# A transformer block with S5 and sparse attention: inputs laid out by the host, the first norm's root by a power on GpSimd

## The chip, the core and the metric

The kernel runs on one core of a Trainium2 chip. The core has five engines that run side by side, each through its own queue in order: TensorE (PE), VectorE (DVE), ScalarE (ACT), GpSimd (POOL) and SyncE (SP), which here only issues transfers. On-chip data lie in SBUF and, for PE's results, in the eight banks of PSUM. The metric is the device time of one execution in microseconds (us), lower is better.

## The reference

One block of a decoder in float32 on 512 tokens of width 1024:

```python
n1 = rmsnorm(h, g_mix)                       # y = x * rsqrt(mean(x*x) + eps) * g
z = n1 @ w_in                                # 1024 x 3864: ssm input, queries, 6 key/value sets, gates, merge
y_ssm = s5_mixer(z[:512], a_re, a_im, log_dt, b, c, d, w_glu)
y_nsa = nsa_mixer(q, kv, gate_logits, ...)   # compressed, selected and window attention, 8 heads
merge = sigmoid(z[1816:])
h = h + (merge[:1024] * (y_ssm @ w_br_ssm) + merge[1024:] * (y_nsa @ w_br_nsa)) @ w_out
h = h + conv_ffn(rmsnorm(h, g_ffn), w_up, conv_w, conv_b, w_down)
h = h + sigmoid(rmsnorm(h, g_ple) @ w_ple_gate) * (p @ w_ple_proj)
out = rmsnorm(h, g_final)
```

The part that matters most here is the start: rmsnorm of x, the product p @ w_ple_proj (the "embedding"), which needs nothing else, the columns of z that hold values and gates, and the parameters of the state space model: dt = exp(log_dt), a_bar = exp(lam * dt) with a complex lam, so that the kernel needs an exponential and the sine and cosine of an angle for each of 32 x 64 states.

## The kernel before

A float32 product is made of three passes in a faster type (helper mm3, lines 83 to 85): each operand is split into a high part, a copy that ACT makes (line 76), and a low part, a subtraction on DVE or POOL (line 55 through `split`). PE multiplies with the contracted dimension on the partitions. So x, p and several small parameter arrays, whose rows lie the other way in memory, are turned by PE transposes through PSUM.

The order of the first stage is written out by hand for PE, ACT and DVE, in a `manual_schedule` block (lines 365 to 441); POOL's order, and the order of all later work, comes from a planner that places each instruction by its own estimate of when it is ready. `issue_after(x)` queues what is traced inside it behind x on x's engine. In the first stage stand:

- g_mix, a row, is spread over the partitions by two products with ones (L368); prow (three parameter rows of the model), drow and p (pin) are transposed (L371, L381, L376).
- The embedding, matmuls `embedded(i, qt)` (L351) with 512 columns, for two halves i of w_ple_proj and four blocks qt of 128 tokens, three passes of two each: 48 in all. `embedded_out` copies the sums from PSUM to SBUF on ACT. The names `acc` and `o` are two PSUM banks each, taken in turn by `either()`.
- Norm 1, for each block: the sum of squares of its rows on ACT (L309; for block 0 half of it on DVE, L388); the root `rstd_of` (lines 120 to 136) as seven or nine small DVE steps; `x_scaled` (L316 on, recorded at L64) multiplies x by the root and by g_mix, on DVE; eight transposes (L324); `t_high` copies the high part n1h from PSUM on ACT; `t_low` makes the low part n1l on DVE from PSUM.
- `v_passes(qt, ...)` (L298): for each block 24 matmuls with 280 columns, which make the values of two attention branches and the gates from n1 and WV; `v_out` takes them out of PSUM (L305 for the gates).
- `u_split` prepares the first two weight tiles of w_in.

Behind that block PE makes four projections `proj` (L83 to L85, group `pj`) for the model's input, eight more for queries, compressed and plain keys, and interleaves the model's own matmuls in four quarters (`ssm_quarter`).

The model's parameters: step exponential `exp_of` with tag e0 and the angles (kk, fl) run on POOL; a second exponential, tag e1, gives rho, also on POOL; both are chains of operations on 128 x 16 elements. On POOL a fused multiply-add is two instructions (`stg`). Behind `trig_at` (the last DVE instruction traced before, that is t_low of block 2), DVE makes sines and cosines (L507 to L536), powers PR and PI, the coefficients bb from B (braw); POOL makes the tables `tab` (L55 in group tab). C (craw) is turned by two groups of four transposes (L591), the gains of the later norms and the compression's position terms by L580 and L582, and the convolution's weights and bias (crow) by four (L1132) at 316 us, between projection matmuls late in the attention stage.

Weights come in tiles of 512 KB by `wraw` (L187), three buffers in turn, on SP's DMA queue. A tile of w_in or w_up is read in pieces of 512 B, the others in pieces of 1 or 2 KB; B is read in pieces of 64 B, C in pieces of 256 B and twice, so that it stands on both halves of the partitions.

Of the kernel before, what the change touches and what calls it, by code (L numbers as in the profile page):

```python
# [18 lines left out]
P = 128  # L19
T = 512  # L20
# [25 lines left out]
def hybrid_kernel(ctx: ExitStack, tc: tile.TileContext, A, out):  # L46
# [186 lines left out]
    sX = ExitStack()
    px = sX.enter_context(pool("x", 1, "right"))
    xall = slot(cp, "h16", [P, NQ, D], F32, "xall")
    xts = [xall[:, qt] for qt in range(NQ)]
    sq = px.tile([P, D], F32, name="sq")
    wv0 = slot(py, "y8", [P, 2, KD, P], F32, "wv0")
    grow = wv0[0:1, 1].rearrange("p a b -> p (a b)")
    ones = pP.tile([1, P], F32, name="ones")  # L240
    G.memset(ones, 1.0)
    grow2 = pP.tile([2 * KD, P], F32, name="grow2")
    gains = cp.tile([P, 2, KD], F32, name="gains")

    def xload(qt):
        nc.sync.dma_start(xts[qt], dr("x", qt * P * D, [[D, P], [1, D]]))


    pin = slot(pa, "v4", [P, NQ, PLE], F32, "pin")
# [5 lines left out]
    def wpload(i):  # L255
        nc.sync.dma_start(wpr[:, i], dr("w_ple_proj", i * 512, [[D, P], [P * D, 2], [1, 512]]))

    nc.sync.dma_start(grow, dr("g_mix", 0, [[D, 1], [1, D]]))
    nc.sync.dma_start(pin, dr("p", 0, [[PLE, P], [P * PLE, NQ], [1, PLE]]))
# [3 lines left out]
    xload(1)  # L263
    nc.scalar.dma_start(dlog, dr("ssm_log_dt", 0, [[2, NPAIR], [1, 2]]))
    nc.scalar.dma_start(prow[:, 0], dr("ssm_a_re", 0, [[P, NPAIR], [1, P]]))
    nc.scalar.dma_start(prow[:, 1], dr("ssm_a_im", 0, [[P, NPAIR], [1, P]]))
    nc.scalar.dma_start(drow, dr("ssm_d", 0, [[P, 4], [1, P]]))
# [3 lines left out]
    VCOLS = ((OFF_KV + 384, 0, P, wv0[:, 0]),  # L271
             (OFF_KV + 640, P, P + 24, slot(py, "t8", [P, KD, P + 24], F32, "wv1")))
    for c0, w0, w, raw in VCOLS:
        nc.sync.dma_start(raw, dr("w_in", c0, [[INW, P], [P * INW, KD], [1, w]]))
    for qt in range(2, NQ):
        xload(qt)
    uraw = [wraw("w_in", INW, 0, ct * P, KD, P) for ct in range(2)]
    for i, nm in enumerate(("g_ffn", "g_ple")):
        nc.sync.dma_start(grow2[i * KD:(i + 1) * KD], dr(nm, 0, [[P, KD], [1, P]]))
# [5 lines left out]
    def wv(x, i):  # L285
        _, w0, w, raw = VCOLS[i]
        return WV[:, x, :, w0:w0 + w], raw
# [20 lines left out]
    def squared(qt):  # L308
        S.activation(sq, xts[qt], AF.Square, accum_out=ss4[:, qt:qt + 1])  # L309

    G.tensor_copy(prow[:, 2].rearrange("p (g s) -> p g s", g=2), dlog[:, :, None].to_broadcast([NPAIR, 2, HD]))
    prm = pP.tile([P, 3, NPAIR], F32, name="prm")

    def x_scaled(qt, r):
        for i, x in enumerate(halves(xts[qt])):
            stt(x, x, r, gbs[i], MUL, MUL)  # L316

    def t_high(qt):

        res = []  # L320
        for b in range(2):
# [1271 lines left out]
```

## Time and profile before

| what | value |
|---|---|
| median of 3 runs (lowest, highest) | 819.1 us (818.9, 819.38) |
| span of the profiled execution, first to last instruction | 817.2 us |
| so outside that span, by the median | 1.9 us |
| PE busy in that span | 802.4 us, 98% |
| DVE, ACT, POOL busy | 523.2, 401.2, 252.0 us |
| instructions | 12276 |
| transfers | 87.85 MB, 114305 packets, 97733 of them between 512 B and 2 KB |
| mean granted PE clock | 0.997 |

The profile is of one execution. L12 stands for line 12 of the kernel; a line can be that of a helper, so that groups are told apart by the names of their tiles. "Busy" for PE counts a pipelined matmul to its modelled end, so that a busy PE is not always at its peak; the step from one start to the next tells its rate.

### The profile page before, as it was taken

How to read it: one execution, taken by the hardware profiler on the slowest of the kernel's cores; microseconds unless marked ns; L12 is line 12 of the kernel's file. 1: busy time of each engine (PE TensorE's matmuls, PEld its weight loads, DVE VectorE, ACT ScalarE, POOL GpSimd, SP SyncE). 2: the span in 40 equal slices, each digit the busy share in tenths (PEclk: the TensorE clock that was granted, in tenths of full speed). 3: DMA queues.
4: the chain of work that ended last, by engine and by line, in shares of the span. 5: the costliest groups of instructions: out<-in, count | busy, mean ns of one | idle time of the engine just before them, and what ended most of it. 6: DMA issues, size and time to landing. Idle time of an engine off the chain costs nothing. (4 is left out here: it accounts for less than half of the span.)

```text
span 817.2 us, 12276 instructions
## 1 busy us (share of the span) xinstructions
PE 802.4 (98%) x4523; PEld 674.4 (83%) x4523; DVE 523.2 (64%) x1085; ACT 401.2 (49%) x746; POOL 252.0 (31%) x309
## 2 busy tenths in 40 slices
PE   8999999999999999999999999999999999999995
PEld 5977888888888888878898888888888888888884
DVE  4899888756777742296444444555444757898764
ACT  5548364435877653334354344444444433484632
POOL 6477021015645444141032322333333200000321
PEclk9999999999999999999999999999999999999998
DMA  9937232422333413345033233332332352525111
GB/s 295 271 102 181 69 88 54 105 78 81 100 78 78 155 53 83 103 154 155 1 92 108 86 102 103 104 96 86 102 99 84 102 177 80 206 67 167 51 52 51
DMA packets 114305, 87.85 MB, mean 108 GB/s; under 512 B 9921, under 2 KB 97733, under 8 KB 114246
## 3 DMA queue, kind: packets, MB, share of 16 engines
q1 hardware_dynamic: 113566, 86.02, 36.5%
q10 hardware_dynamic: 680, 1.07, 0.3%
q8 instruction: 35, 0.57, 0.3%
q14 instruction: 24, 0.20, 0.1%
HBM read 77.63 MB, written 5.24 MB: 101 GB/s over the span
## 5 line engine op out<-in xcount | busy, mean ns | idle before, releaser
L55 POOL TENSOR_TENSOR wl<-wr,wh 128x1024 fp32r<-128x1024 f32 x39 | 93.9, 2407 | 250.0 <-ACT wh L76 249.9
L76 ACT ACTIVATE wh<-wr 128x1024 fp32r<-128x1024 f32 x88 | 93.2, 1059 | 96.8 <-issue 29.2
L55 DVE TENSOR_TENSOR wl<-wr,wh 128x1024 fp32r<-128x1024 f32 x49 | 63.5, 1297 | 56.4 <-ACT wh L76 56.4
L83 PE MATMUL pj<-n1h,wh 128*128 128x512 f32 x224 | 91.0, 406 | 0.6 <-ACT gates L305 0.6
L85 PE MATMUL pj<-n1h,wl 128*128 128x512 f32 x224 | 88.1, 394 | 0.8 <-DVE wl L55 0.8
L84 PE MATMUL pj<-n1l,wh 128*128 128x512 f32 x224 | 87.9, 392 | 0.0
L64 DVE SCALAR_TENSOR_TENSOR cv<-ub,cvp,cv 128x511 f32<-128x511 f32 (+1 forms) x44 | 32.9, 748 | 66.2 <-ACT cv L1272 65.5
L84 PE MATMUL ua<-n2l,wh 128*128 128x512 f32 (+1 forms) x176 | 66.9, 380 | 0.2 <-DVE n2l L64 0.2
L83 PE MATMUL ua<-n2h,wh 128*128 128x512 f32 (+1 forms) x176 | 66.9, 380 | 0.0
L85 PE MATMUL ub<-n2h,wl 128*128 128x512 f32 (+1 forms) x176 | 66.8, 379 | 0.0
L83 PE MATMUL ub<-n2h,wh 128*128 128x512 f32 (+1 forms) x176 | 66.8, 379 | 0.0
L84 PE MATMUL ub<-n2l,wh 128*128 128x512 f32 (+1 forms) x176 | 66.8, 379 | 0.0
L85 PE MATMUL ua<-n2h,wl 128*128 128x512 f32 (+1 forms) x176 | 66.8, 379 | 0.0
L85 PEld LDWEIGHTS pj<-n1h,wl 128*128 128x128 f32 x224 | 42.1, 188 | 10.7 <-DVE wl L55 1.6
L83 PEld LDWEIGHTS pj<-n1h,wh 128*128 128x128 f32 x224 | 42.1, 188 | 8.4 <-ACT gates L305 0.8
L61 POOL TENSOR_SCALAR pr<-pr,su,gates 128x512 f32<-128x512 f32 (+1 forms) x64 | 39.1, 622 | 31.4 <-DVE su L983 28.9
L84 PEld LDWEIGHTS pj<-n1l,wh 128*128 128x128 f32 x224 | 42.2, 188 | 7.5 <-issue 0.4
L55 DVE TENSOR_TENSOR pl<-ptp,ph 128x128 fp32r<-128x128 f32 (+1 forms) x64 | 31.2, 488 | 15.1 <-ACT ph L76 14.7
L55 POOL TENSOR_TENSOR wg1l<-wr,wg1h 128x1024 fp32r<-128x1024 f32 x2 | 4.8, 2424 | 113.6 <-ACT wg1h L76 113.6
L982 ACT ACTIVATE pr<-pr,nb 128x512 f32<-128x512 f32 (+1 forms) x64 | 35.6, 557 | 7.6 <-DVE nb L980 7.5
L76 ACT ACTIVATE ph<-ptp 128x128 fp32r<-128x128 f32 (+1 forms) x64 | 27.7, 433 | 22.8 <-PE ptp L991 22.3
L84 PEld LDWEIGHTS ua<-n2l,wh 128*128 128x128 f32 x176 | 33.1, 188 | 6.7 <-DVE n2l L64 0.4
(500 smaller groups left out, 2077.3 us busy)
## 6 DMA issues: line engine op xcount, KB each, us to landing
wr<-in_w_up_dram SPq DMA_DIRECT2D x44, 512.0 KB, 4.0
wr<-in_w_in_dram SPq DMA_DIRECT2D x28, 512.0 KB, 3.9
b<-in_w_down_dram SPq DMA_DIRECT2D x14, 512.0 KB, 3.7
QQ<-QT SPq DMA_DIRECT2D x16, 256.0 KB, 3.6
wr<-in_w_out_dram SPq DMA_DIRECT2D x8, 512.0 KB, 3.5
wr<-in_w_down_dram SPq DMA_DIRECT2D x8, 512.0 KB, 4.8
wr<-in_w_ple_gate_dram SPq DMA_DIRECT2D x8, 512.0 KB
xall<-in_x_dram SPq DMA_DIRECT2D x4, 512.0 KB
```

Source lines behind the costliest of these rows:

```text
L55: e.tensor_tensor(o, a, b, op=op)
L61: e.tensor_scalar(o, a, s1, s2, op0=op0, op1=op1)
L64: e.scalar_tensor_tensor(o, a, s, b, op0=op0, op1=op1)
L76: S.activation(o, a, AF.Copy)
L83: PE.matmul(ps, lh, rh, start=start, stop=False)
L84: PE.matmul(ps, lh, rl, start=False, stop=False)
L85: PE.matmul(ps, ll, rh, start=False, stop=stop)
L982: S.activation(pp, pp, AF.Exp, bias=nb, scale=-1.0, accum_out=su)
```

## The change

Six things change together.

1. The host hands over copies with another order of the same numbers (`laid_out`). Weight tiles lie in memory as they are loaded, so each partition reads one piece. x comes twice: as rows (for the squares and for the residual) and as x_t, blocks with the model dimension on the partitions. p comes transposed. All parameters that were transposed by PE come as one array of columns, `cols`; B and C as one array `bc`, C already on both halves. The value and gate columns of w_in come as `w_v`.
2. The transposes of x, p, prow, drow, grow2, perow, craw and crow go, with g_mix's spread and their copies from PSUM.
3. Norm 1 works on x_t: x_gain multiplies by g_mix on POOL; rooted, on POOL, adds the two sums, takes the power -0.5 and multiplies a unit matrix by the result; spread, on PE, multiplies that diagonal by a constant matrix, so that each token's root stands on all partitions, in PSUM; x_scaled, n_high and n_low follow on DVE, ACT and DVE.
4. POOL's order in the first stage is written by hand as well.
5. The step exponential and the angles move from POOL to DVE: five steps before the squares of block 0, 21 behind them. The second exponential stays on POOL, queued behind the low part of the second half of w_ple_proj.
6. The order of the block is new (the lines that the old order had are left out below): first passes of the embedding go over all four blocks, all three value passes of a block stand together, v_out of block 0 and 1 come earlier.

```diff
 def wraw(name, ld, row0, c0, kt, c, raw=None):
...
-        nc.sync.dma_start(raw, dr(name, row0 * ld + c0, [[ld, P], [P * ld, kt], [1, c]]))
+        n = (row0 // (kt * P)) * (ld // c) + c0 // c
+        nc.sync.dma_start(raw, dr(name, n * P * kt * c, [[kt * c, P], [c, kt], [1, c]]))
...
+    cols = cp.tile([P, NCOLS], F32, name="cols")
+    gmix, gains, dcol, prm, pes, cvp = (cols[:, a:b] for a, b in zip(COLS, COLS[1:]))
...
+    bcraw = pP.tile([P, 4, NPAIR, 16], F32, name="bcraw")
+    root = px.tile([P, P], F32, name="root")
+    G.memset(root, math.sqrt(D))
+    half = px.tile([P, 1], F32, name="half")
+    G.memset(half, -0.5)
     def xload(qt):
-        nc.sync.dma_start(xts[qt], dr("x", qt * P * D, [[D, P], [1, D]]))
+        nc.sync.dma_start(rows[qt], dr("x", qt * P * D, [[D, P], [1, D]]))
+        nc.sync.dma_start(xT[:, qt], dr("x_t", qt * P * D, [[D, P], [P, KD], [1, P]]))
...
+    nc.scalar.dma_start(cols, dr("cols", 0, [[NCOLS, P], [1, NCOLS]]))
+    for k in range(2):
+        nc.sync.dma_start(pin[:, k], dr("p_t", k * T, [[2 * T, P], [1, T]]))
     wpload(0)
     xload(0)
     wpload(1)
-    xload(1)
...
+    for w0, w, raw in VCOLS:
+        nc.sync.dma_start(raw, dr("w_v", P * KD * w0, [[KD * w, P], [w, KD], [1, w]]))
+    for qt in range(1, NQ):
         xload(qt)
     uraw = [wraw("w_in", INW, 0, ct * P, KD, P) for ct in range(2)]
...
+    def x_gain(qt):
+        tt(xT[:, qt], xT[:, qt], gm8, MUL, G)
+    def rooted(qt, s2=0.0):
+        r = small("rx")
+        ts(r, ss4[:, qt:qt + 1], s2, D * EPS, ADD, ADD, G)
+        tt(r, r, half, ALU.pow, G)
+        dgs[qt] = px.tile([P, P], F32, name="dg", tag="dg", bufs=1)
+        ts(dgs[qt], ident, r, None, MUL, None, G)
+    def spread(qt):
+        if not rbp:
+            rbp[0] = bank("s", "rb")
+        PE.matmul(rbp[0][:, qt * P:(qt + 1) * P], root, dgs[qt], start=True, stop=True)
+    def x_scaled(qt):
+        tt(xT[:, qt], xT[:, qt], rbp[0][:, None, qt * P:(qt + 1) * P].to_broadcast([P, KD, P]), MUL)
+    def n_high(qt):
+        copy(n1h[n_of(qt)], xT[:, qt])
+    def n_low(qt):
+        tt(n1l[n_of(qt)], xT[:, qt], n1h[n_of(qt)], SUB)
...
+    def angles():
+        ts(lre, prm[:, 0], -1e-4, None, ALU.min)
+        yield
+        yield from exp_of(dt, prm[:, 2], "e0", V)
+        tt(lr, lre, dt, MUL)
+        yield
+        tt(th, aim, dt, MUL)
+        yield
+        C0 = 2 * math.pi / 4096
+        c1 = math.floor(C0 * 2 ** 18) / 2 ** 18
+        c2 = math.floor((C0 - c1) * 2 ** 29) / 2 ** 29
+        c3 = C0 - c1 - c2
+        ts(kk, th, 1.0 / C0, MAGIC, MUL, ADD)
+        yield
+        ts(kk, kk, MAGIC, None, SUB)
+        yield
+        stt(fl, kk, -c1, th, MUL, ADD)
+        yield
+        stt(fl, kk, -c2, fl, MUL, ADD)
+        yield
+        stt(fl, kk, -c3, fl, MUL, ADD)
+        yield
+        ts(fl, fl, 1 / (2 * math.pi))
+        yield
+        ts(rd, kk, 1 / 4096.0, MAGIC, MUL, ADD)
+        yield
+        ts(rd, rd, MAGIC, None, SUB)
+        yield
+        stt(kk, rd, -4096.0, kk, MUL, ADD)
+        yield
...
+    with tc.manual_schedule(engines={mybir.EngineType.PE, mybir.EngineType.Activation, mybir.EngineType.DVE,
+                                    mybir.EngineType.Pool}):
         for k in range(2):
+            copy(pT[0][:, k], pin[:, k])
+            tt(pT[1][:, k], pin[:, k], pT[0][:, k], SUB)
+        angled = angles()
+        for _ in range(5):
+            next(angled)
+        for k in range(2):
+            copy(wp[0][:, 0, k], wpr[:, 0, k])
         tt(wp[0][:, 1], wpr[:, 0], wp[0][:, 0], SUB)
+        x0 = halves(rows[0])
+        S.activation(x0[0], x0[0], AF.Square, accum_out=ss4[:, 0:1])
+        V.tensor_tensor_reduce(out=x0[1], in0=x0[1], in1=x0[1], scale=1.0, scalar=0.0, op0=MUL, op1=ADD,
                                accum_out=ss4[:, NQ:])
+        x_gain(0)
+        rooted(0, ss4[:, NQ:])
+        for n in range(2):
+            for k in range(2):
+                for qt in range(NQ):
+                    embedded(0, qt, (n,), (k,))
         copy(wp[1][:, 0], wpr[:, 1])
+        copy(*wv(0, 0))
+        for _ in angled:
+            pass
+        spread(0)
+        x_scaled(0)
         tt(wp[1][:, 1], wpr[:, 1], wp[1][:, 0], SUB, G)
+        exp_at = last(mybir.EngineType.Pool)
+        for qt in range(NQ):
+            embedded(0, qt, (2,))
         for qt in range(2):
             embedded_out(0, qt)
+        squared(1)
+        rooted(1)
+        x_gain(1)
+        n_high(0)
+        wv_lo(0)
+        n_low(0)
         for qt in (2, 3):
             embedded_out(0, qt)
+        for qt in range(3):
+            embedded(1, qt)
         squared(2)
+        V.tensor_copy(*wv(0, 1))
+        spread(1)
+        embedded(1, 3)
+        embedded_out(1, 0)
+        x_scaled(1)
+        n_high(1)
+        rooted(2)
+        x_gain(2)
+        wv_lo(1)
+        n_low(1)
         squared(3)
+        for qt in (1, 2):
             embedded_out(1, qt)
+        v_passes(0, (0, 1, 2))
+        spread(2)
+        x_scaled(2)
+        n_high(2)
+        rooted(3)
+        x_gain(3)
+        embedded_out(1, 3)
+        n_low(2)
         trig_at = last(mybir.EngineType.DVE)
+        v_passes(1, (0, 1, 2))
         u_split(0, 0)
+        spread(3)
+        x_scaled(3)
+        v_passes(2, (0, 1, 2))
+        n_high(3)
+        n_low(3)
         u_split(0, 1)
+        v_out(0)
         u_split(1, 0)
         zero_at = last(mybir.EngineType.Activation)
+        u_split(1, 1)
+        v_out(1)
         v_passes(3, (0, 1, 2))
         for qt in (2, 3):
             v_out(qt)
...
+    with tc.issue_after(exp_at):
+        for _ in exp_of(rho, lr, "e1", G):
+            pass
...
-    with tc.issue_after(first_v):
-        ppe = bank("s", "ppe")
-        PE.transpose(ppe[:, 32:32 + 2 * KD], grow2, ident[:2 * KD, :2 * KD])
...
+        copy(FL[:, i, :, :, NCMP - 1], pes[:, i, :, None].to_broadcast([P, 16, 2]))
+        S.activation(CT[:, i], bcraw[:, 2 + i], AF.Copy, scale=(1.0, -1.0)[i])
...
-    for i in range(4):
-        PE.transpose(ps[:, i * 44:(i + 1) * 44], crow[:, i], ident[:44, :44])
-    V.tensor_copy(cvp.rearrange("p a b -> p (a b)"), ps[:, :176])
...
+def laid_out(i):
+    def tiles(w, kt, c):
+        k, n = w.shape
+        return w.reshape(k // (kt * P), kt, P, n // c, c).transpose(0, 3, 2, 1, 4)
...
+        "x_t": x.reshape(NQ, P, KD, P).transpose(0, 3, 2, 1),
+        "p_t": i["p"].reshape(T, 2, P).transpose(2, 1, 0),
+        "cols": np.concatenate(cols, 1),
+        "bc": np.stack(bs + cs, 1),
```

More of the change, by code (lines that the diff above doesn't have):

```diff
@@ L308, in squared, with n_of @@
     def squared(qt):
[L309 to L321, printed above, removed]
-            ps = bank("t", "nt")
-            for k in range(4):
-                PE.transpose(ps[:, k * P:(k + 1) * P], xts[qt][:, (4 * b + k) * P:(4 * b + k + 1) * P], ident)
-            o = (slice(None), slice(4 * b, 4 * b + 4), slice(qt * P, qt * P + P))
-            res.append((o, ps.rearrange("p (k t) -> p k t", k=4)))
-            copy(n1h[o], res[-1][1])
-        return res
-    def t_low(res):
-        for o, ps in res:
-            tt(n1l[o], ps, n1h[o], SUB)
+        S.activation(rows[qt], rows[qt], AF.Square, accum_out=ss4[:, qt:qt + 1])
+    gm8 = gmix[:, :, None].to_broadcast([P, KD, P])
+    rbp = {}
+    dgs = {}
+    def x_gain(qt):
[12 more added lines that the diff above has]
+        tt(xT[:, qt], xT[:, qt], rbp[0][:, None, qt * P:(qt + 1) * P].to_broadcast([P, KD, P]), MUL)
+    def n_of(qt):
+        return (slice(None), slice(None), slice(qt * P, qt * P + P))
+    def n_high(qt):
+        copy(n1h[n_of(qt)], xT[:, qt])
+    def n_low(qt):
+        tt(n1l[n_of(qt)], xT[:, qt], n1h[n_of(qt)], SUB)
     uw = []
@@ L349, in embedded @@
         for n in passes:
-            for k in range(2):
+            for k in ks:
                 PE.matmul(pjb[i, qt], pT[int(n == 1)][:, k, qt * P:(qt + 1) * P], wp[i][:, int(n == 2), k], start=n + k == 0,
@@ L363, in embedded_out @@
         copy(pjo[i, qt], pjb[i, qt])
-    with tc.manual_schedule(engines={mybir.EngineType.PE, mybir.EngineType.Activation, mybir.EngineType.DVE}):
-        gbs = [bank("s", f"gb{i}") for i in range(2)]
-        for ps, g in zip(gbs, halves(grow)):
-            PE.matmul(ps, ones, g, start=True, stop=True)
-        pps = bank("t", "pps")
-        for i in (2, 0, 1):
-            PE.transpose(pps[:, i * 16:(i + 1) * 16], prow[:, i], ident[:NPAIR, :NPAIR])
-        copy(prm.rearrange("p a b -> p (a b)"), pps[:, :48])
-        for k in range(2):
-            ps = bank(either(), "ptr")
-            for qt in range(NQ):
-                PE.transpose(ps[:, qt * P:(qt + 1) * P], pin[:, qt, k * P:(k + 1) * P], ident)
-            copy(pT[0][:, k], ps)
-            tt(pT[1][:, k], ps, pT[0][:, k], SUB)
-        copy(wp[0][:, 0], wpr[:, 0])
-        tt(wp[0][:, 1], wpr[:, 0], wp[0][:, 0], SUB)
-        PE.transpose(pps[:, 48:52], drow, ident[:4, :4])
-        copy(dcol, pps[:, 48:52])
-        for n in range(3):
-            for qt in range(2):
-                embedded(0, qt, (n,))
-        x0 = halves(xts[0])
-        S.activation(sq[:, :512], x0[0], AF.Square, accum_out=ss4[:, 0:1])
-        V.tensor_tensor_reduce(out=sq[:, 512:], in0=x0[1], in1=x0[1], scale=1.0, scalar=0.0, op0=MUL, op1=ADD,
-                               accum_out=ss4[:, NQ:])
-        x_scaled(0, rstd_of(ss4[:, 0:1], ss4[:, NQ:]))
-        copy(wp[1][:, 0], wpr[:, 1])
@@ L1579 @@
     arrays, args = {}, {}
-    for name in _INS:
-        a = _np.ascontiguousarray(inputs[name])
+    for name, a in laid_out(inputs).items():
+        a = _np.ascontiguousarray(a)
         arrays[f"in_{name}_dram"] = a
```

202 lines of the change are left out of this document (66 added, 136 removed).

## The prediction

> **What bounds the kernel now.** I read the page, then busy time by stretch, who PE waited for, and PE in order of time.
>
> ```profile
> span 817.2 us, 12276 instructions
> PE 802.4 (98%) x4523; PEld 674.4 (83%) x4523; DVE 523.2 (64%) x1085; ACT 401.2 (49%) x746; POOL 252.0 (31%) x309
> ```
> ```profile
> 0.00:10.00 10.00, 6.08 (x16) 3.47 (x17) 1.40 (x3) 3.69 (x7) 3.89 (x28) 1.00 0.78 275
> 10.00:40.00 30.00, 30.00 (x184) 27.11 (x185) 26.22 (x72) 19.02 (x38) 18.59 (x56) 1.00 1.11 287
> 40.00:80.00 40.00, 38.57 (x230) 30.80 (x230) 36.90 (x86) 25.15 (x52) 30.93 (x59) 1.00 0.55 143
> 80.00:400.00 320.00, 320.00 (x2164) 270.70 (x2163) 213.70 (x523) 167.18 (x364) 102.20 (x98) 1.00 0.33 92
> 400.00:800.00 400.00, 399.63 (x1877) 334.80 (x1876) 236.69 (x381) 182.22 (x281) 92.51 (x65) 1.00 0.33 100
> ```
> After the stretch and its length stand PE, PEld, DVE, ACT and POOL busy, granted clock, DMA share and GB/s. From 10 to 800 us PE is idle for 1.8 us in all, with DMA at a third after 80 us. The rearranged weights of the later stages are therefore priced at nothing: PE's own work hides their loads, and without that cover a load's saving (0.5 us, from the transfer rates below) would count once per load. The change gains only what it takes from PE, or from PE's waits, and nearly all of that lies before 60 us.
>
> ```profile
> 10.00 2.07 PE L351 MATMUL pje<-wp,pTh 128*128 128x512 f32 x4 [1.44 <-ACT dcol L76]
> 11.87 1.91 PE L351 MATMUL pje<-wp,pTl 128*128 128x512 f32 x4
> 13.58 1.30 PE L351 MATMUL pje<-wp,pTh 128*128 128x512 f32 x4
> 14.72 1.04 PE L324 MATMUL nt<-ident,xall 128*128 128x128 f32 x8
> 15.51 0.70 PE L351 MATMUL pje<-wp,pTh 128*128 128x512 f32 x2
> ...
> 25.85 1.19 PE L298 MATMUL vps<-WV,n1l 128*128 128x280 f32 x8
> 26.88 1.20 PE L298 MATMUL vps<-WV,n1h 128*128 128x280 f32 x8
> ...
> 39.03 0.23 PE L580 MATMUL ppe<-ident,grow 16*128 16x16 f32 x1
> ...
> 39.73 0.48 PE L83 MATMUL pj<-n1h,wh 128*128 128x512 f32 x1
> ```
> Columns: start, length, then what ran. Embedding starts at 10.00 and first steps by 0.43 us a matmul (11.87 to 13.58, four). A value matmul steps by 0.129 (25.85 to 26.88, eight), eight transposes of x take 0.79 (14.72 to 15.51), and the first projection starts at 39.73. The question is where that start goes.
>
> **The change, part by part.** *PE.* Out of the first stage: four groups of transposes of x (3.2 us), 0.70 of ppe and cps (39.03 to 39.73), and all that stands before 10.00. In: four spreads. Their nearest row is four fp32 products of 128 columns, eight passes, in 1.06 us:
>
> ```profile
> 76.69 1.06 PE L718 MATMUL wps<-Uc,WB 128*128 128x128 f32 x8
> ```
> That is 0.27 each; the bounds are 0.22 (the same without the last one's tail) and 0.5 (with a stop at each change of operand type). I take 0.35, so 1.4.
>
> *Transfers.* These rows have the columns of the second fence.
>
> ```profile
> 5.00:10.00 5.00, 3.56 (x14) 2.31 (x13) 1.40 (x3) 2.40 (x6) 2.42 (x10) 1.00 1.03 394
> 20.00:25.00 5.00, 5.00 (x28) 4.16 (x27) 3.39 (x7) 3.60 (x9) 4.02 (x12) 1.00 1.14 129
> ```
> The first holds p, w_ple_proj and x, in pieces of 1 KB and more; the second B and C, in pieces of 64 and 256 B. The new loads all have long pieces, so 394 GB/s holds throughout and 512 KB take 1.33 us. x comes twice: 2 MB more. Counting SP's queue in order (the first 785 KB by 5 us, as before) with 0.7 us for the last packets gives: w_ple_proj half 0 at 6.7, rows of x 0 at 8.0, x_t 0 at 9.4, half 1 at 10.7, w_v at 12.0 and 13.6, then rows and x_t in turn at 14.9, 16.3, 17.6, 18.9, 20.3, 21.6, the first u weights at 22.9. ACT issues one DMA for four, ahead of its work.
>
> *Engines.* For each 128 tokens: a square on ACT; on POOL x_gain (two inputs, 1024 columns), an add, a power and a diagonal; the spread; x_scaled on DVE from PSUM; n_high on ACT; n_low on DVE, whose inputs now both lie in SBUF.
>
> ```profile
> L55 POOL TENSOR_TENSOR wl<-wr,wh 128x1024 fp32r<-128x1024 f32 x39 | 93.9, 2407 | 250.0 <-ACT wh L76 249.9
> L76 ACT ACTIVATE wh<-wr 128x1024 fp32r<-128x1024 f32 x88 | 93.2, 1059 | 96.8 <-issue 29.2
> L55 DVE TENSOR_TENSOR wl<-wr,wh 128x1024 fp32r<-128x1024 f32 x49 | 63.5, 1297 | 56.4 <-ACT wh L76 56.4
> ```
> ```profile
> 12.98 0.22 POOL L55 TENSOR_TENSOR e0q<-gtFalse,e0r 128x16 f32<-128x16 f32 x1
> 13.29 0.25 POOL L59 TENSOR_SCALAR gtFalse<-e0q 128x16 f32<-128x16 f32 x1
> 13.50 2.38 POOL L55 TENSOR_TENSOR wp<-wpr,wp 128x1024 fp32r<-128x1024 f32 x1
> ```
> x_gain is 2.4, x_scaled and n_low 1.2 each, a copy on ACT 1.0 (0.53 for 512 columns). No row has a power. From below it is 0.22 (a multiply), from above 2.4 (the longest POOL row); as its one column is nearest to the short rows I take 0.4, so add, power and diagonal take 1.1. The step exponential and angles (26 small operations) go to DVE: five early, 21 behind the squares. Their price, and what they wait for, shows here:
>
> ```profile
> 381.43 2.41 POOL L55 TENSOR_TENSOR wl<-wr,wh 128x1024 fp32r<-128x1024 f32 x1 [18.92 <-ACT wh L76]
> ```
> ```profile
> 382.38 1.47 DVE L64 SCALAR_TENSOR_TENSOR rt<-ry,rv 128x1 f32<-128x1 f32 x1
> 383.88 0.16 DVE L64 SCALAR_TENSOR_TENSOR rt<-rt 128x1 f32<-128x1 f32 x1
> 384.08 0.16 DVE L64 SCALAR_TENSOR_TENSOR ry<-rt,ry 128x1 f32<-128x1 f32 x1
> 384.27 0.22 DVE L64 SCALAR_TENSOR_TENSOR rt<-ry,rv 128x1 f32<-128x1 f32 x1
> ```
> A chained small step costs 0.2. But the one at 382.38 took 1.47 and ended at 383.85, with POOL's multiply (383.84): a DVE operation with two SBUF inputs stands still while POOL streams. So each x_gain and the low half of w_ple_proj block the angles, wv_lo and n_low, and the reverse.
>
> *The walk.* PE starts at 7.3 (half 0 copied). Sixteen matmuls, nine at 0.43 and seven at 0.23, end at 12.9. POOL has x_gain 9.4 to 11.8, the root until 12.9, the spread follows at once, then the low half of w_ple_proj until 15.1. PE does twenty more and stands at 17.8 before embedded(1, 2): its bank is freed by embedded_out(0, 2), which ACT holds behind n_high(0), behind x_scaled(0), behind the 21 angles. These start at 9.6, need 4.2 us, lose 4.3 to POOL and end at 18.1. x_scaled, n_high and the copy-out make it 20.9: PE stands 3.1 us. Six matmuls, a spread and six more reach 24.0; two passes of values 26.1. The third needs wv_lo, whose parts stand behind x_gain(1) (18.5 to 20.9) and x_gain(2) (24.0 to 26.3) and end at 27.7: 1.6 more. Then 1.0 ends block 0; spread and 3.1 for block 1 end at 32.2, spread and 3.1 for block 2 at 35.7, block 3 at 38.8. x_gain(3) (29.6 to 32.0), x_scaled(3) and n_high(3) (35.3) just precede it.
>
> So the first projection moves from 39.73 to 38.8: -0.9. If POOL's second exponential, which may stand in the gaps before the roots, gets all its 26 steps in there, 8.6 us at 0.33, it is 42 to 43.
>
> *Behind it*, on PE:
>
> ```profile
> 45.28 0.60 PE L591 MATMUL cps<-ident,craw 128*128 128x128 f32 x4
> 46.49 0.50 PE L83 MATMUL pj<-n1h,wh 128*128 128x512 f32 x1 [0.60 <-ACT gates L305]
> ```
> ```profile
> PE pj L85 <- DVE wl L55: 0.8, 1, 0.8
> ```
> ```profile
> 315.56 0.39 PE L84 MATMUL pj<-n1l,wh 128*128 128x512 f32 x1
> 315.79 0.39 PE L85 MATMUL pj<-n1h,wl 128*128 128x512 f32 x1
> 316.11 0.44 PE L1132 MATMUL cvps<-ident,crow 44*128 44x44 f32 x4
> 316.48 0.50 PE L83 MATMUL pj<-n1h,wh 128*128 128x512 f32 x1
> ```
> The transposes of C go: 46.49 - 45.28 = 1.21, of which 0.60 is a wait for v_out on ACT that stands in the new order too; I take 0.6 and half the wait, 0.9. Half of the 0.8 us wait for wl: 0.4. The transposes of conv_w go: 316.48 - 315.79 less one step of 0.23 = 0.5. The sum is -0.9 - 0.9 - 0.4 - 0.5 = -2.7 us: the profiled span from 817.2 to 814.5, and, since the runs' median of 819.1 stands 1.9 above that span, **816.4 us**.
>
> **The rivals.**
> (a) *PE stays dense*: the angles slip into gaps and no wait remains. Then 7.3, 48 embedding matmuls at 0.23 (11.0) and 1.8 for nine slow ones, four spreads (1.4), 96 value matmuls at 0.129 (12.4): first projection at 33.9, -5.8 in place of -0.9, **811.5**. For it: PE is never idle from 10 to 45 now. Against it: the 1.47 us row.
> (b) *POOL's queue becomes the bound, slower than before.* POOL runs in order. If steps of the second exponential, which wait for the delayed angles, stand ahead of the roots, or the power costs over 1.2 us, the roots of blocks 2 and 3 come 3 us or more later than walked (block 3's after 30), and the spreads hold PE's queue with all value matmuls behind them. With the first projection at 42.5 to 43.5 (+3.3), the 0.5 of conv and 0.6 of C off and no wait saved, it is +2.2: **821.3**. Against: POOL has about 16 us of written work between 9 and 30.
> (c) *The wait moves to the SSM preparation.*
> ```profile
> 31.84 0.28 DVE L55 TENSOR_TENSOR ang<-kk,mt 128x128 f32<-128x128 f32 x1
> 43.16 0.52 POOL L55 TENSOR_TENSOR tab<-tab,COS 128x16 f32<-128x16 f32 x2 [10.66 <-DVE COS L55]
> 64.03 0.49 PE L710 MATMUL wbps<-ident,Z 128*128 128x128 f32 x3
> ```
> The tables start behind n_low(2), which the walk ends at 32.9 against 31.84 now, with more DVE work left, so POOL's tables and the first transpose of Z (64.03) come no earlier than now. If PE reaches that transpose early and has too little else, what was gained before it is lost and only conv's 0.5 stays: **818.6**. For it: DVE is busy 36.9 of 40 us there. Against: projections still unissued can fill.
> (d) *PE goes slow again in the 3.1 us gap.* Nine matmuls at 0.43 for 0.23, as at 10.00, add 1.8: **818.2**. The Trainium skill ("TensorE: Matmul & The Clock Gate", HAM oscillation) says that a gap beyond about 3.4 us halves the clock; by that rule a gap only a little longer than the one walked decides. This profile grants full clock from 10 to 800 us but has no such gap to show it.
> That the change doesn't do what it says would be short pieces left in its loads; with x still doubled that is (b) by DMA, and small.
>
> **How the numbers follow.** Forecast 0.34, (a) 0.20, (b) 0.22, (c) 0.14, (d) 0.10. The forecast's own range is 814.4 to 818.6 (walk from 36.8 to 41, by power 0.22 to 1.2, spreads, and where POOL's steps stand). The measurement can tell about 0.2%, 1.6 us: 817.5 to 820.7 is no change. Faster: 0.25 of the forecast, all of (a), 0.03 of (d), so 0.48; same: 0.09 of the forecast, most of (c) and (d), so 0.28; slower: (b) and what is left of (c), 0.24. The range, 811 to 821.5, takes in (a) and (b) at their centres.
>
> **What would show it.** Embedding from about 7.3; a 16-column DVE angle of 1 to 2 us ending with x_gain or the low half of w_ple_proj; a PE gap near 18 ended by ACT's copy-out, none if (a), longer and ended by POOL's diagonal if (b); the first w_in matmul at 38.8; no stop at L591 and L1132's places; in (d), steps of 0.43 behind the gap; in (c), PE idle at the Z transposes. I am wrong if a DMA ends a PE wait after 12 us, if the power is far from 0.4, or if PE's time behind 80 us changes by over 1 us.

## The result: 826.15 us, slower than before

The changed kernel takes 826.15 us (median of 4 runs, 824.63 to 826.56) against 819.0 us (818.73 to 819.38) for the kernel before, measured on the same chip: a ratio of 1.0086, 95% interval 1.0072 to 1.0101. The prediction said 816.4, range 811 to 821.5: the wrong side, and outside the range. The profiled execution took 826.31 us with a span of 824.6, against 817.2 before.

PE's time in stretches of the span, first of the changed kernel, then of the kernel before (columns: from and to; length and PE's busy time with its instructions; granted clock, 1.00 is full; share of the DMA engines; GB/s):

```profile
10.00:40.00 30.00, 25.28 (x132) 0.94 0.87 334
40.00:80.00 40.00, 34.04 (x151) 0.91 0.36 119
80.00:400.00 320.00, 320.00 (x2220) 1.00 0.31 96
```
```profile
10.00:40.00 30.00, 30.00 (x184) 1.00 1.11 287
40.00:80.00 40.00, 38.57 (x230) 1.00 0.55 143
80.00:400.00 320.00, 320.00 (x2164) 1.00 0.33 92
```

Behind 80 us nothing is lost: PE is dense from there in both. The loss lies ahead of it, as idle time and as a lower clock. PE's waits in the changed kernel (what waited, for what; total, times, longest):

```profile
PE pje L415 <- ACT wp L75: 8.2, 1, 8.2
PE pj L82 <- ACT gates L295: 5.4, 1, 5.4
PE pje L415 <- ACT wv L75: 2.1, 1, 2.1
```

The first is the start. The largest of the others is one that the prediction didn't have: 5.4 us ahead of the first projection, ended by `gates` on ACT. PE's timeline around it (start, length, what ran, idle time before it and what ended that):

```profile
21.17 0.73 PE L415 MATMUL pje<-wp,pTh 128*128 128x512 f32 x2 [2.05 <-ACT wv L75]
...
41.52 1.19 PE L288 MATMUL vps<-WV,n1h 128*128 128x280 f32 x8
48.10 0.79 PE L82 MATMUL pj<-n1h,wh 128*128 128x512 f32 x1 [5.39 <-ACT gates L295]
...
52.94 0.39 PE L84 MATMUL pj<-n1h,wl 128*128 128x512 f32 x1
```

The values end at 42.7, but the first projection starts at 48.10 (39.73 before), and its first eleven steps, to 52.94, take 4.84 us where eleven at 0.228 take 2.5. So the first projection is 8.4 us late, and another 2.3 go to the low clock. From the first projection to the end it is 776.5 us against 777.5, with those 2.3 in it: without them the parts behind the first stage became 3.3 us cheaper, where 1.8 were forecast. 8.4 - 1.0 is the 7.4 us by which the span grew.

Who held `gates`? ACT's timeline at that place:

```profile
41.99 0.19 ACT L295 ACTIVATE gates<-vps 128x24 f32<-128x24 f32 x1 [2.65 <-DVE VV L54]
42.08 1.05 ACT L75 ACTIVATE wh<-wr 128x1024 fp32r<-128x1024 f32 x1
43.02 0.38 ACT L75 ACTIVATE VV<-vps 128x256 fp32r<-128x256 f32 x1
43.29 1.15 ACT L677 ACTIVATE Z<-ident 128x512 f32<-128x512 f32 x2
...
46.62 1.35 ACT L677 ACTIVATE CX<-ident 128x640 f32<-128x640 f32 x2
47.87 0.18 ACT L295 ACTIVATE gates<-vps 128x24 f32<-128x24 f32 x1
```

Eight copies that only write zeros into Z and CX (four rows of two, the first and the last are shown) stand between the copy of VV(1) and gates(1), the last reader of the PSUM bank that the first projection takes. They are queued behind `zero_at`. That line is in both versions, and the diff shows it unchanged; but before, v_out(0) and v_out(1) stood ahead of it, and in the new order v_out(1) stands behind it. The list of changes says that v_out of block 0 and 1 come earlier. For block 1 the opposite is so: it moved behind `zero_at` and, on DVE, behind the low half of the second u weight.

### The profile page after: what moved, and what is told of

Same layout as the page of the kernel before. It is cut to its first block, busy times and chain, and to the rows that moved or that the text cites. A ratio compares the mean times of both kernels' runs of the same rounds, so it can differ in the third digit from the quotient of the medians.

```text
span 824.6 us, 12105 instructions
## 1 busy us (share of the span) xinstructions
PE 796.2 (97%) x4468; PEld 669.7 (81%) x4468; DVE 525.4 (64%) x1078; ACT 403.9 (49%) x741; POOL 258.6 (31%) x286
## 3 DMA queue, kind: packets, MB, share of 16 engines
q10 hardware_dynamic: 720, 1.19, 0.4%
## 5 line engine op out<-in xcount | busy, mean ns | idle before, releaser
L63 DVE SCALAR_TENSOR_TENSOR cv<-ub,cols,cv 128x511 f32<-128x511 f32 (+1 forms) x44 | 32.9, 748 | 66.2 <-ACT cv L1272 65.5
L82 PEld LDWEIGHTS pj<-n1h,wh 128*128 128x128 f32 x224 | 42.7, 190 | 13.7 <-ACT gates L295 5.6
```

Of the source, the lines that this page charges most:

```text
L63: e.scalar_tensor_tensor(o, a, s, b, op0=op0, op1=op1)
L82: PE.matmul(ps, lh, rh, start=start, stop=False)
```

## The experiments

All numbers are medians; ratios are against the kernel before, run beside each. Theory A: the order on ACT cost the 5.4 us and with it the clock. Rival B: the first stage itself. Each experiment builds on the one named in it.

### One edit at a time on ACT's order

```diff
         u_split(0, 1)
         v_out(0)
+        v_out(1)                  # e2, e3
         u_split(1, 0)
-        zero_at = last(mybir.EngineType.Activation)    # e1, e3
         u_split(1, 1)
-        v_out(1)                  # e2, e3
         v_passes(3, (0, 1, 2))
         for qt in (2, 3):
             v_out(qt)
+        zero_at = last(mybir.EngineType.Activation)    # e1, e3
```

> The changed kernel with one edit: the eight zero fills of Z and CX on ACT may start only behind the last v_out, not behind the copy of the second u weight. Theory A (ACT's order: the first projection of u waits for its PSUM bank, which gates(1) on ACT still reads, and gates(1) stands behind the zero fills from 43.29 to 47.87): gates(1) is then held only by Vector's low half of VV(1), which ended at 45.33, so the first projection starts at about 45.6 in place of 48.10, PE's wait falls from 5.39 to about 2.9 us, and the time falls by 2.5 us to about 823.6, by up to 2 us more if PE's clock no longer halves behind the shorter gap. Theory B (the first stage up to 42 us is what made the kernel slow, and PE would wait for something else there): the time stays at 826.

> The changed kernel with v_out(1) written ahead of the copy and the low half of the second u weight; the zero fills keep their place behind that copy, so they now stand between v_out(1) and v_out(3). Theory A: VV(1) and gates(1) are done by 42.6, and the first projection follows the values at about 42.8 without a wait. Its 24 steps at 0.23 end near 48.3; the second projection takes the other bank, which gates(3) frees: the zero fills end near 48.5, and gates(3) comes near 50.2, so PE loses about 2 us there instead of 5.39. Sum about -5.4 + 2 and -2 for the slow clock that is saved: 820 to 822.5. Theory B: 826.

> The changed kernel with both edits: v_out(1) ahead of the second u weight, the zero fills behind the last v_out. Theory A: the first projection at about 42.8, its first steps at 0.23 and not at 0.43, no wait for gates: -5.4 for the wait and about -2.1 for the eleven slow steps, so about 818.7, the time of the kernel before within 0.2%. Theory B: 826. A rival C: the zero fills now come late enough for the first Z transposes, and PE waits there instead: 820 to 823.

Measured: e1 821.9 us (ratio 1.0037, interval 1.0024 to 1.0049), e2 823.49 (1.0055, 1.0042 to 1.0069), e3 819.09 (1.0002, 0.9994 to 1.0011). PE's and ACT's timeline in e1, then PE's in e2 and in e3:

```profile
44.73 0.74 PE L82 MATMUL pj<-n1h,wh 128*128 128x512 f32 x1 [2.90 <-ACT gates L295]
...
44.49 0.19 ACT L295 ACTIVATE gates<-vps 128x24 f32<-128x24 f32 x1 [1.97 <-DVE VV L54]
```
```profile
42.66 0.50 PE L82 MATMUL pj<-n1h,wh 128*128 128x512 f32 x1
...
50.36 0.50 PE L82 MATMUL pj<-n1h,wh 128*128 128x512 f32 x1 [1.95 <-ACT un L75]
...
63.76 0.50 PE L84 MATMUL pj<-n1h,wl 128*128 128x512 f32 x1 [1.78 <-DVE wl L54]
```
```profile
41.94 0.50 PE L82 MATMUL pj<-n1h,wh 128*128 128x512 f32 x1 [0.69 <-ACT gates L295]
```

The waits are those that A named: 2.90 in e1, none at the first projection and 1.95 at the second in e2, 0.69 in e3. So the fills made 2.5 us of the 5.39, and v_out(1)'s place 2.2: in e1 gates(1) still waits for the low half of VV(1), which DVE makes behind that of the second u weight. e1 lies in its range (about 7 slow steps were left of 11). e2 came out 1 us above its own: the zero fills also held back a weight's copy on ACT, and the 1.78 us for wl had not been counted. e3 takes back 7.1 us by order alone, without one operation more or less. In the two profiles, 7.4 us apart, 1.3 of it is that PE could start earlier (6.91 against 8.16), which the order does not make. B falls for these 7 us; rival C (a wait at Z) did not appear.

### The clock's part

```diff
         v_passes(3, (0, 1, 2))
+        for n in range(38):
+            PE.matmul(rbp[0][:, :280], n1h[:, 0, :P], WV[:, 0, 0], start=True, stop=True)
         for qt in (2, 3):
```

> The changed kernel with 38 matmuls of 128x280 whose results nobody reads, written behind the last value matmul; they fill 4.9 of the 5.4 us in which PE stands before the first projection. Nothing else differs. Theory A with the clock: the first projection still starts near 48.1, since gates(1) has not moved, but its first steps take 0.23 and not 0.43 us, which saves about 2.1 us: 824.0. If the clock has no part in the loss: 826.1.

Measured: 824.41 us (1.0068, 1.0055 to 1.008), 1.7 below the changed kernel. PE's timeline:

```profile
41.12 5.06 PE L510 MATMUL rb<-WV,n1h 128*128 128x280 f32 x38
46.70 0.51 PE L82 MATMUL pj<-n1h,wh 128*128 128x512 f32 x1 [0.52 <-ACT gates L295]
...
66.47 0.50 PE L84 MATMUL pj<-n1h,wl 128*128 128x512 f32 x1 [1.76 <-DVE wl L54]
```

The wait for gates(1) still ends at the same distance from PE's start (46.70 - 6.80 against 48.10 - 8.16, 39.9 both times), but the steps behind it are full speed. PE's idle time had thus cost twice: once as a wait, and 2.3 us more as slow steps. What this is worth to the whole kernel is not shown: in the two profiles PE's earlier start makes 1.4 of the 1.7 us, and from the first projection to the end e4 takes 776.2 us against 776.5. The waits for wl took most of the saving back (2.4 us in all; the changed kernel had 0.6).

### What holds the first stage: the port, the angles, POOL's queue

With e3 the first projection starts at 41.94; the walk had 38.8. Two edits of e3, and both at once:

```diff
     def x_scaled(qt):                                   # e5, e7 (x_gain is not called)
-        tt(xT[:, qt], xT[:, qt], rbp[0][:, None, qt * P:(qt + 1) * P].to_broadcast([P, KD, P]), MUL)
+        for k in range(KD):
+            stt(xT[:, qt, k], xT[:, qt, k], gmix[:, k:k + 1], rbp[0][:, qt * P:(qt + 1) * P], MUL, MUL)
...
-        for _ in angled:                                # e6, e7
-            pass
         spread(0)
...
         n_low(1)
+        for _ in angled:
+            pass
```

> e3_both, with the gain of norm 1 moved off POOL: its four multiplies of 1024 columns go, and x_scaled becomes eight Vector operations of 128 columns that multiply by the gain column and by the spread root at once (about 1.7 us in place of 1.2). Theory D (POOL's multiplies hold the port that Vector's operations with two SBUF inputs need, and x_scaled waits for them: 2.37 us before block 1's, 2.38 before block 2's, and n_low(2) stretched to 2.88): x_scaled(1) starts near 21 in place of 23.6, block 3's value matmuls end near 36 to 38, and the first projection starts 4 to 5 us earlier than the 41.9 of e3_both: 814 to 816.5. Theory E (the first stage is bound by Vector's own work or by ACT, and the POOL multiplies are covered): Vector has 2 us more to do, the time is that of e3_both, 819, or 1 us above it.

> e3_both, with the 21 angle operations on Vector written behind n_low(1) and no longer ahead of x_scaled(0). Theory F (the prediction's own step: the 21 angles ahead of x_scaled(0) hold the embedding's bank, and so PE's gap near 18 us): x_scaled(0) starts near 13 in place of 16.9, n_high(0) follows the square of block 1 near 16.3, PE's wait of 1.3 to 2.1 us ended by ACT's wv copy is gone, and with x_gain(1) no longer delayed by blocked POOL operations x_scaled(1) starts about 2.5 us earlier: 816 to 817.5. Rival: the angles only move, and stand in front of x_scaled(2) instead, where Vector waits for POOL's x_gain(2) anyway: the gain at block 1 is kept by half, 818; if they come out on top of that wait, 819 to 820.

> Both of the last two edits on e3_both: the gain on Vector inside x_scaled, and the 21 angles behind n_low(1). If D and F both hold, the first projection starts near 36 and the time is 812.5 to 815. If only D holds, as e5_gain_dve. If Vector's own work is the bound (theory E), 819 or above. The tables of the SSM preparation start behind n_low(2) in every one of these; if they become the bound, PE waits before the first transposes of Z and e7 is no faster than e5.

Measured: e5 816.71 us (0.9971, interval 0.996 to 0.9983), e6 821.24 (1.0028, 1.0017 to 1.0039), e7 818.17 (0.9987, 0.9978 to 0.9996). In e5 x_scaled(1) starts at 21.91, 1.6 us earlier than in e3, and the first projection 2.2 us earlier:

```profile
39.74 0.50 PE L82 MATMUL pj<-n1h,wh 128*128 128x512 f32 x1 [0.81 <-ACT gates L295]
```

D holds, with about half the gain expected. The edit removes POOL's use of the port and DVE's wait for POOL's product together, so their shares are not separated by it. One long POOL operation was left, and it still cost an angle 2.2 us, as DVE's timeline of e5 shows, then POOL's:

```profile
11.69 2.42 DVE L60 TENSOR_SCALAR kk<-th 128x16 f32<-128x16 f32 x1
```
```profile
11.68 2.40 POOL L54 TENSOR_TENSOR wp<-wpr,wp 128x1024 fp32r<-128x1024 f32 x1 [0.38 <-ACT wp L75]
```

e6 shows half of F: PE's wait ended by ACT's wv copy is gone from its table of waits. But moved in one piece the 21 angles stand in front of x_scaled(2), and a spread writes the bank that x_scaled(2) reads. PE in e6 and in e7:

```profile
33.89 0.77 PE L320 MATMUL rb<-dg,root 128*128 128x128 f32 x2 [4.64 <-DVE xT L54]
34.88 2.24 PE L288 MATMUL vps<-WV,n1h 128*128 128x280 f32 x8 [0.23 <-ACT n1h L75]
```
```profile
31.06 0.46 PE L320 MATMUL rb<-dg,root 128*128 128x128 f32 x2 [2.71 <-DVE xT L63]
```

The step that held the embedding's bank was named rightly; taking it away there gave more back at another place (4.64 us, and eight matmuls in 2.24 us where 1.19 is full speed). The side of the rival, 819 to 820, was nearer.

### Undoing one part

```diff
-    G.memset(root, math.sqrt(D))                        # e8
+    G.memset(root, 1.0)
...
-        r = small("rx")
-        ts(r, ss4[:, qt:qt + 1], s2, D * EPS, ADD, ADD, G)
-        tt(r, r, half, ALU.pow, G)
+        r = rstd_of(ss4[:, qt:qt + 1], s2)
...
-        yield from exp_of(dt, prm[:, 2], "e0", V)       # e12
+        yield from exp_of(dt, prm[:, 2], "e0", G)
```

> e3_both with one part of the change undone: the root is again the chain of ten small operations on Vector (add, shifted bits, two refinement steps), POOL keeps the diagonal and the gain. The power on POOL took 0.57 us and its add 0.3; the chain costs Vector about 2 us for each of the four blocks, in its queue ahead of wv_lo and n_low, and its operations have two SBUF inputs, so POOL's multiply can block them. If the power is a gain, this is 2 to 5 us slower than e3_both: 821 to 824. If Vector has room there, 819.

> e3_both with one part of the change undone: the step exponential stands on POOL again (20 operations at about 0.31, 6.2 us, of which 18 stand behind the first diagonal). The angles that follow on Vector then end near 20 in place of 16.8, x_scaled(0) and the embedding's bank come 3 to 4 us later, and POOL's low half of w_ple_proj stands behind the exponential: 821.5 to 824. Rival: the 2.8 us that Vector lost to POOL's multiply at 9.57 are saved by it, and the two cancel: 819.

Measured: e8 830.17 us (1.0131, 1.0117 to 1.0145), e12 825.9 (1.0094, 1.008 to 1.0108): 11.1 and 6.8 us above e3, beyond both ranges. In this order of the first stage both parts are worth far more than expected. In e8 the chain stands in DVE's queue, so each diagonal is late, and so is what DVE has behind it. PE's waits in e8:

```profile
PE rb L318 <- POOL dg L58: 4.4, 3, 2.6
PE pj L84 <- DVE wl L54: 2.9, 1, 2.9
PE pje L413 <- ACT wv L75: 2.9, 1, 2.9
```

In e12 PE waited for the low half of w_ple_proj, which stands behind the exponential on POOL:

```profile
20.95 2.08 PE L415 MATMUL pje<-wp,pTh 128*128 128x512 f32 x4 [4.63 <-POOL wp L54]
```

Behind that gap the granted clock is half from 19.35 to 29.59 us, so e12's price is in part the clock's.

### The last long POOL operation, the angles divided, v_out early

```diff
-        tt(wp[1][:, 1], wpr[:, 1], wp[1][:, 0], SUB, G)       # e9, on e5
+        tt(wp[1][:, 1], wpr[:, 1], wp[1][:, 0], SUB)          # on DVE, behind the angle th
...
+        for _ in range(4):                                    # e10, on e9: three angles before x_scaled(0),
+            next(angled)                                      # four here, two before n_low(2);
         x_scaled(1)                                           # second exponential on POOL behind rooted(2)
...
+        for qt in range(2):                                   # e11, on e10: copies here, low halves behind
+            v_high(qt)                                        # them, gates behind n_low(3)
         v_passes(2, (0, 1, 2))
         n_high(3)
```

> e5_gain_dve with the last long POOL multiply of the first stage moved too: the low half of w_ple_proj's second part is a Vector operation (1.2 us) between the angles, no longer a POOL operation of 2.4 us. Theory D (the port): in e5 one angle took 2.42 us at 11.69 under that POOL operation; without it the angles end near 14.9 with the 1.2 us included, x_scaled(0) starts 0.7 us earlier than 15.6, and PE's wait of 1.7 us near 19 falls to about 1: 816.0. If the port is not what stretched the angle, x_scaled(0) starts near 16.8, 1.2 us later than in e5: 817.5 to 818.

> e9_wp_dve with the last nine angles divided over Vector's idle places: three ahead of x_scaled(0), four ahead of x_scaled(1), two ahead of n_low(2); POOL's second exponential starts only behind the diagonal of block 2. e7 showed that 21 angles in one piece ahead of x_scaled(2) make spread(3) wait 2.7 us on PE (it writes the bank that x_scaled(2) still reads). Divided, x_scaled(0) starts when spread(0) is done (near 13.7), PE's wait near 19 goes, x_scaled(2) starts near 25.5, and the first projection starts near 37.5 to 38.5 in place of 39.74: 814 to 815.5. Rival: Vector's own sum of work is the bound, and the first projection stays at 39.7: 816.7.

> e10_angles_split with v_out(0) and v_out(1) divided: their copies on ACT stand ahead of n_high(3), their low halves on Vector ahead of n_low(3), their gates ahead of the low half of the first u weight. The wait of 0.8 us that the first projection still has for gates(1) goes: 0.8 us below e10, 813.3 to 814.7. Rival: ACT's copies delay n_high(3), and PE waits there instead: as e10.

Measured: e9 816.93 us (0.9983, 0.9974 to 0.9992), e10 815.98 (0.9966, 0.9954 to 0.9979), e11 816.84 (0.9978, 0.9969 to 0.9987). e9 and e11 gave nothing. In e9 x_scaled(0) starts at 14.61, 1.0 us earlier than in e5, and the angle behind th takes 0.17 us again: it was POOL's long operation that had stretched it, as D says (16.8 was expected if not). The wait near 19 did go, but the second diagonal came later (1.81 us, from PE's timeline):

```profile
21.90 0.49 PE L320 MATMUL rb<-dg,root 128*128 128x128 f32 x2 [1.81 <-POOL dg L58]
```

In e11 the wait for gates(1) went and PE waited 1.40 and 0.75 us later for ACT's and DVE's copies of finished projections, under another order of the planner's. e10's ratio is 0.0005 below that of e5, with intervals that overlap: less than was expected. It kept a wait for POOL's queue. Its POOL timeline, then PE's:

```profile
29.85 1.63 POOL L58 TENSOR_SCALAR dg<-ident,rx 128x128 f32<-128x128 f32 x1
```
```profile
31.54 0.49 PE L320 MATMUL rb<-dg,root 128*128 128x128 f32 x2 [1.98 <-POOL dg L58]
```

### POOL's order, and where its gain went

e13 (on e10) and e14 (on e3) let the second exponential start behind root 3; e15 (on e14) and e16 (on e13) also put the two operations that square rho behind the last v_out on DVE.

```diff
         rooted(3)
+        exp_at = last(mybir.EngineType.Pool)                  # e13, e14
...
-    tt(rho4, rho, rho, MUL)                                   # e15, e16
-    tt(rho4, rho4, rho4, MUL)
+    with tc.issue_after(rho_at):                              # the last DVE instruction of v_out(3)
+        tt(rho4, rho, rho, MUL)
+        tt(rho4, rho4, rho4, MUL)
```

> e10_angles_split with POOL's second exponential issued only behind the diagonal of block 3. In e10 the add of root 3 stood at 28.44 behind twelve of its operations and its diagonal ended at 31.48, and PE waited 1.98 us at 31.54 for it (rival b of the prediction, POOL's queue, inside the improved first stage). Behind the roots, diagonal 3 ends before PE asks for it near 29.6, and the first projection starts up to 2 us earlier: 814 to 815. Rival: rho comes near 37 instead of 34, and Vector's tables or ACT's n_high(3) take the place of the wait: 816.

> e3_both with the same edit alone: the gain and the low half of w_ple_proj stay on POOL, the second exponential starts behind root 3 and its multiply. Rival b of the prediction (POOL's queue order is what sets the roots): root 1 comes 1.2 us earlier (its add stood at 17.60 for a sum of squares that was ready at 16.4), the diagonals and x_gain 1 to 3 follow, and the first projection starts 1 to 2 us earlier than 41.94: 817 to 818.3. If the multiplies of the gain and the port are what holds the blocks (theory D), and not the order: 819.1 within 0.7.

Measured: e13 817.19 us (0.9977, 0.9967 to 0.9988), e14 819.27 (1.0002, 0.9994 to 1.0011). By the time alone, rival b would have fallen. The traces say otherwise: in e14 the first projection starts at 39.62, 2.3 us earlier than in e3, and PE's next wait is new. PE's timeline of e14 and the cause, on DVE:

```profile
46.98 0.50 PE L82 MATMUL pj<-n1h,wh 128*128 128x512 f32 x1 [1.62 <-ACT gates L295]
```
```profile
42.11 0.18 DVE L54 TENSOR_TENSOR rho<-rho 128x16 f32<-128x16 f32 x1 [2.77 <-POOL rho L54]
```

rho is now later on POOL, and an operation of 0.18 us at the head of DVE's queue stops all that stands behind it for 2.77 us. In e13 the same operation stands before n_low(3) (idle 2.19) and PE waits 2.38 us for n1l.

> e14_exp_order with the two small Vector operations that square rho written behind the last v_out. In e14 the first projection came 2.3 us earlier than in e3 (39.62 against 41.94), but the first of the two stood at the head of Vector's queue for 2.77 us until POOL's rho was done (42.11), the low halves of VV(2) and of the u weight behind it, and PE lost 1.62, 0.26 and 0.76 us at the next projections. If that is where the gain went: 816.8 to 817.8, PE's wait for gates(3) near 47 under 0.3. If PE's later work is bound otherwise (the SSM tables): 819.2 as e14.

> e13_exp_last with the same edit. There the squaring of rho stood before n_low(3) on Vector for 2.19 us, and PE waited 2.38 us at 36.72 for n1l and then ran a few steps slow. Without it the first projection starts near 38 in place of 40.3: 814 to 815. If the gain is taken back behind it: 816 to 817.

Measured: e15 816.32 us (0.9968, interval 0.9955 to 0.998), e16 814.34 (0.9943, interval 0.993 to 0.9957). PE at the first projection in e15, then in e16:

```profile
37.49 1.19 PE L288 MATMUL vps<-WV,n1h 128*128 128x280 f32 x8
39.42 0.50 PE L82 MATMUL pj<-n1h,wh 128*128 128x512 f32 x1 [0.74 <-ACT gates L295]
```
```profile
37.24 0.50 PE L82 MATMUL pj<-n1h,wh 128*128 128x512 f32 x1 [0.86 <-ACT gates L295]
```

e15 came out 0.5 us below its range, without a wait for gates(3); e16 lies in its own. e15 has the changed kernel's operations, each on its engine, in another order, and is 9.8 us faster than it and 2.5 faster than the kernel before. e16, with the gain and one low half on DVE and the angles divided, is the fastest: 4.5 us below the kernel before by the medians of the same call (814.34 against 818.8).

## Why the prediction was wrong, point by point

**The step that failed** is the last one of the walk and the first of "Behind it". The walk ended with x_scaled(3) and n_high(3), which "just precede" the first projection, and put that projection right behind block 3's values. So it priced the wait for the projection's PSUM bank at nothing. "Behind it" looked at v_out on ACT at one place only, ahead of the second projection, where the kernel before waits 0.60 us for gates(3), took that wait as one "that stands in the new order too", and counted half of it. ACT's queue was not walked past n_high(3). There gates(1), which frees the first projection's bank, stands behind two copies (the second u weight, VV(1)) and eight zero fills, and it needs DVE's low half of VV(1): PE waited 5.39 us, and 2.3 more went to the half clock behind that gap. At the second projection it waited for nothing. The diff was enough to see it: v_out(1) had moved to the other side of `zero_at`. With the two lines moved (e3) 7.1 us come back.

**The gap and the clock.** The gap at embedding(1, 2) and its chain were right: ended by ACT's copy-out (recorded as `wv`) at 21.17, walked 20.9, 2.05 long and not 3.1, since PE got there later. Rival (d) was given 0.10 with a condition on this gap; the clock did fall behind this gap, and again in the 5.39 that the walk didn't have (rows in the last section).

**The port.** Walked: 4.3 us of the angles lost, end at 18.1. Measured: two angles stood still, 3.8 us lost, end at 18.40. Its rows on DVE (the third is n_low(2), behind x_gain(3)):

```profile
10.41 1.86 DVE L63 SCALAR_TENSOR_TENSOR e0r<-e0n,e0r 128x16 f32<-128x16 f32 x1
...
14.02 2.30 DVE L63 SCALAR_TENSOR_TENSOR dt<-e0q,e0s 128x16 f32<-128x16 f32 x1
...
33.45 2.88 DVE L54 TENSOR_TENSOR n1l<-xT,n1h 128x1024 fp32r<-128x1024 f32 x1 [1.12 <-ACT n1h L75]
```

The 1.6 us stall for wv_lo did not come; the same mechanism stopped n_low(2) and cost PE 1.43 at 36.38. What was not walked is the reverse, which the prediction names in two words ("the reverse"): DVE stops POOL. The diagonal of block 1, priced inside 1.1 for add, power and diagonal, is the second row of POOL here:

```profile
12.63 0.57 POOL L54 TENSOR_TENSOR rx<-rx,half 128x1 f32<-128x1 f32 x1
...
20.73 2.24 POOL L58 TENSOR_SCALAR dg<-ident,rx 128x128 f32<-128x128 f32 x1
```

In the three rows above the DVE operation has two SBUF inputs, as the prediction says; e5's at 11.69 has one and stood still too.

**The power** took 0.57, not 0.4. With add and diagonal it is 1.7 (12.23 to 13.92), 0.6 more than the sum had; no PE wait ended on it in block 0.

**The first stage as a whole.** Values ended at 42.7 where 38.8 was walked. The stalls on the way sum to 4.5 us (2.05, 0.60, 1.43, 0.41), and 4.7 were walked, at other places. Of the difference of 3.9, 0.9 is the later start (8.16 for 7.3; it lies between 6.65 and 8.81 over the profiles of these runs, so one profile tells it to 1 us), 1.7 are 3.4 us at half clock, and about 1.5 stays. Most of that is in the values: without their stalls the four blocks take 14.3 us where 13.2 were walked. In e15 the values end at 38.7. Counted from PE's start, the first projection was walked at 31.5 us; it came at 39.9, in e3 at 35.0, in e5 at 32.7, in e15 at 32.6 and in e16 at 30.5.

**Rival (b)**, POOL's queue, was real but not what decided: taken away alone (e14) it moves the first projection by 2.3 us, and the time by nothing, because its own follower, rho, takes the place. The first projection passed the 42.5 to 43.5 that (b) had, but through ACT's queue. **(a)** asked for angles that cost nothing; e16 comes nearest with a first projection at 37.24 where (a) had 33.9 (in e11 its first step runs at 35.46, between the value passes of block 3). **(c)** did not appear in any run: no PE wait at the Z transposes.

**Behind the first projection** the three savings were forecast at 0.9, 0.4 and 0.5, together 1.8. From the first projection to the end it is 777.5 us before and 814.6 - 39.42 = 775.2 in e15: 2.3. PE in e15 is 0.3 us ahead of the kernel before at the first projection (39.42 against 39.73), 2.1 at the first `glu` matmul (173.89 against 176.00) and 2.8 at the first `wo` matmul (358.12 against 360.90): 1.8 for the first two terms, forecast at 1.3, and 0.7 at and near the transposes of conv_w, forecast at 0.5. **No DMA** ended a PE wait behind 12 us, and PE's time behind 80 us changed by less than 1 us, as said.

So e15 stands 2.5 below the kernel before, where the sum had -2.7, but in an order that the sum's writer had not chosen. That the two figures are close is in part luck: the first projection gains 0.3 in place of 0.9, and the parts behind it more than forecast.

## What to carry to other kernels

When an edit moves an instruction, look for marks in the text that stay where they are, and ask on which side of each mark the instruction was and is: what is queued behind the mark is now ahead of it. Walk each in-order queue until the last reader of the next PSUM bank has run, not until the last producer. An experiment whose time doesn't move can still have removed a wait; find the wait that took its place (here one 0.18 us operation at the head of a queue) before the theory is dropped.

## What the runs showed of the hardware that was not expected

**The granted clock and the length of a gap.** In every trace here, once the clock has first reached full, it changes only at whole multiples of 3.41 us after that (in the changed kernel at 11.93, 22.17, 25.58, 46.06 and 52.89 us). PE's rows, cut at these multiples (from and to; length and PE's busy time with its instructions; granted clock; DMA share; GB/s): the changed kernel, then e9 (gap of 1.81 us ending at 21.90), then e8 (gap of 2.93 ending at 21.18).

```profile
18.76:22.17 3.41, 1.36 (x6) 1.00 1.02 418
22.17:25.58 3.41, 3.41 (x10) 0.50 1.04 398
42.65:46.06 3.41, 0.06 (x1) 1.00 0.43 153
46.06:49.48 3.42, 1.38 (x3) 0.50 0.38 144
```
```profile
19.88:23.29 3.41, 1.59 (x8) 1.00 1.03 418
23.29:26.71 3.42, 3.42 (x16) 0.50 1.05 394
```
```profile
15.92:19.34 3.42, 2.32 (x11) 1.00 1.03 422
19.34:22.75 3.41, 1.57 (x6) 1.00 1.03 418
```

A gap of 1.81 us was followed by half clock, one of 2.93 was not, so the length of a gap alone does not decide. e8's gap is divided by the boundary at 19.34. What the clock goes with is PE's idle time in one such stretch. Over all 18 traces, a stretch at full clock with 2.03 us idle or more was followed by half clock each time, one with 1.76 or less never, and of four in between (1.81 to 1.86) two were. Idle times in one stretch add up: in e2 gaps of 0.48 and 1.44 us gave 1.81 and half clock. The way back took a fuller stretch: 0.93 us idle kept e12 at half clock, and 0.20 let e13 return to full. This is read off the traces; no run here changes only the place of a gap between the boundaries. One order can meet either case: e8's four executions had mean clocks of 0.997 (the profiled one) and 0.989 to 0.991.

The Trainium skill ("TensorE: Matmul & The Clock Gate", HAM oscillation) warns of gaps beyond about 3.4 us; here little more than half of that was enough in some executions. The same page (Part 1: The HAM clock gate) says that activity is judged in windows of 3413 ns that run freely. The boundaries above agree with that.

**The shared port stops both sides, and for the whole instruction.** DVE operations of 0.17 us took 1.86, 2.30 and 2.42; POOL's diagonal of 0.62 took 2.24 (and 3.04 in e5), a sum of one column 1.5 in e14. The Trainium skill ("SBUF — State Buffer", SBUF: two separate sides) calls the pair an exclusive lock held for the full instruction; the rows agree. A power on 128 x 1 took 0.56 to 0.59 on POOL wherever it wasn't stopped so, and 1.39 to 1.97 in four profiles where it was (e3, e4, e5, e16).
